# A hybrid decoder block on one Trainium2 core: moving operands shifted by 64 bytes against the stationary ones

## The chip, the core and the metric

The kernel runs on one NeuronCore of a Trainium2 chip. The metric is the device time of one execution in microseconds (us). The engines are named as in the profile: PE is the matrix engine's matmul stream, PEld its weight loads, DVE the vector engine, ACT the scalar engine, POOL the GpSimd engine, SP the engine that issues most DMAs. SBUF is the on-chip memory of 128 partitions that the engines read their operands from, PSUM the accumulators that PE writes.

## What is computed

One decoder layer on 512 tokens of width 1024, all in float32 (cut to what matters):

```python
h = rmsnorm(x, pre_mix_norm)
q_r, k_r, v_r, g_r, q_s, k_s, v_s, gate_r, gate_s = split(h @ w_in)
y_r = (silu(g_r) * group_norm(retention(q_r, k_r, v_r))) @ w_ret_out
y_s = sliding_window_attention(q_s, k_s, v_s, sinks) @ w_swa_out
merged = sigmoid(gate_r) * y_r + sigmoid(gate_s) * y_s
x = x + rmsnorm(merged @ w_out, post_mix_norm)
h = rmsnorm(x, pre_mlp_norm)
u = square(relu(h @ w_up))                  # the MLP's first product, 1024 -> 4096
x = x + rmsnorm(u @ w_down, post_mlp_norm)  # the MLP's second product, 4096 -> 1024
```

## The kernel before

Every float32 operand of a large product is held as two tiles, a high part (`whi`, `hT0`, `h2c0`, ...) and a low part (`wlo`, `hT1`, `h2c1`, ...), of the type float32r. ACT makes the high part by a copy (L129), DVE the low part by a subtraction (L130). A product of two such pairs is three matmuls (`mm3`, L170 to L175): high by high, high by low, low by high.

```python
170    def mm3(ps, a, b, first, last, more=False):
172        (ah, al), (bh, bl) = a, b
173        nc.tensor.matmul(ps, ah, bh, start=first, stop=False, ...)
174        nc.tensor.matmul(ps, ah, bl, start=False, stop=False, ...)
175        nc.tensor.matmul(ps, al, bh, start=False, stop=last, ...)
```

In each of them `a` is the left operand, a block of 128 columns that is loaded into the array (the profile's LDWEIGHTS, on PEld), and `b` the right or moving operand, whose 256 or 512 columns then stream through it (the MATMUL, on PE). The profile names the moving operand first: `wino<-h2c,whi` is a matmul with moving operand `h2c` and stationary operand `whi`.

The stages, in the order of the program:

1. Projections of the input, attention and retention, 0 to 231 us. `pblk` and `ptok` multiply the input `xg` or the normed input `hT`. `wide` (L602) computes two of the projections with Strassen-Winograd's seven products in place of eight: there the left operands are blocks of `hT` and of the four sums over blocks of `hT`, `hsum` (made once, in `wino_tokens`, L183 to L197), and the right operands are weights of 512 columns. Four of its seven products use `hsum`.
2. The two gates and the output product of the retention (`yr`), 231 to about 355.5 us. A gate (`wino_pair`, L241 to L286, eight calls) is again seven products of 4 x 3 matmuls, here with the weights on the left and 256 columns of the tokens on the right: `hT` in three products, `hsum` in four.
3. The product with `w_out`, up to 400.8 us, with the norms between the sub-layers beside and behind it.
4. The MLP's first product, 400.8 to about 570.7 us. The first three of 16 column blocks are done plainly (`up_half`, L1011), each with moving operands `h2c`, `h2b` and `h2d`, the transposed quarters of the normed activations. The other 13 go through `wino_pair` with `h2c` and `h2d` in three products and the sums `h2s` in four.
5. The MLP's second product (`p`, `p4c`), up to 729 us, with 512 columns at a time; its operands are `left` (stationary) and `whi`, `wlo` (moving).

In `wino_pair` the products stand in a fixed order, and the weights of the next pair are prepared while the present one runs: ACT and DVE split the loaded block (`whi`, `wlo`), two sums are formed on DVE (L223, L224), split in their turn into `p24` (the profile's `p`), and so on. Some of these pieces are held back until ACT has copied a certain PSUM bank (L259, L270, L277), so that the preparation follows PE. The first use of `p24` is the product `s2 t2` (L268), the third of a pair, with moving operand `h2s` in the MLP.

Tiles come out of pools. A pool is a stretch of each partition's memory, and its tiles lie one behind the other in the order of their creation; pools opened later lie behind it (or, with `side="right"`, before it from the far end). So where a tile begins is a matter of everything that was made before it. In the kernel before, a tile `pad` of 72 floats (L303) stands at the far end. In the built program these are the starts of the operand tiles, in bytes of the partition, modulo 512:

```
xg, hT, hsum, wkv, whi, wlo, p24, p22, retT, swaT, wo, mhi, mlo,
h2c, h2b, h2d, h2s, left, tch, rb, s (probabilities), retn, zg     192
pt, kd, qc, st, qk (the retention's own tiles)                     448
ident (the identity, moving operand of the transposes)             128
```

Every slice of these tiles that a matmul reads begins a multiple of 512 bytes further in (256 for one operand of the attention), so the numbers hold for the operands of nearly all matmuls.

Of the kernel before, what the change touches and what calls it, by code (L numbers as in the profile page):

```python
# [10 lines left out]
F32 = mybir.dt.float32  # L11
# [5 lines left out]
P = 128  # L17
# [77 lines left out]
def block_kernel(ctx, tc, x, xT, pre_mix, w_in, w_v, w_g, w_gate, w_ret, w_swa, w_out, sinks, post_mix,  # L95
# [9 lines left out]

    def bank(shape, name="ps"):
        return psum.tile(shape, F32, tag="ps", name=name)

    ident = const.tile([P, P], F32, name="ident")
    make_identity(nc, ident)  # L110
# [69 lines left out]
    def wino_pool(stack, side="left"):  # L180
        return stack.enter_context(tc.tile_pool(name="wx", bufs=1, side=side))
# [59 lines left out]
    def wino_pair(wx, a, b, out, then=None):  # L241

        chain = bank([P, 256], "wino")
        p25 = bank([P, 2, 256], "wino")
        p3 = bank([P, 256], "wino")

        def product(ps, x, y, first=True):  # L250
# [39 lines left out]
    hctx = ExitStack()  # L290
    hpool = hctx.enter_context(tc.tile_pool(name="hpool", bufs=1))
    hT = [hpool.tile([P, KD, SEQ], F32R, name=f"hT{i}") for i in range(2)]
    hsum = [hpool.tile([P, 4, 4, 256], F32R, name=f"hsum{i}") for i in range(2)]

# [3 lines left out]
    sctx = ExitStack()  # L300

    side = ctx.enter_context(tc.tile_pool(name="side", bufs=1, side="right"))
    side.tile([P, 72], F32, name="pad")  # L303
    xTpool = sctx.enter_context(tc.tile_pool(name="xTpool", bufs=1, side="right"))
    xTs = xTpool.tile([P, KD, SEQ], F32, name="xTs", tag="xs")
    xgctx = ExitStack()
# [590 lines left out]

    wctx = ExitStack()
    wpool = wctx.enter_context(tc.tile_pool(name="wpool", bufs=1))
    mctx = ExitStack()  # L900
    mpool = mctx.enter_context(tc.tile_pool(name="mpool", bufs=16))
    fctx = ExitStack()
# [90 lines left out]
    uctx = ExitStack()  # L993
    h2pool = uctx.enter_context(tc.tile_pool(name="h2pool", bufs=1))
    h2spool = uctx.enter_context(tc.tile_pool(name="h2spool", bufs=1))
    h2c = [h2pool.tile([P, 2, 4, 256], F32R, name=f"h2c{i}") for i in range(2)]
    h2d = [h2spool.tile([P, 4, 256], F32R, name=f"h2d{i}") for i in range(2)]
    h2s = [h2spool.tile([P, 4, 4, 256], F32R, name=f"h2s{i}") for i in range(2)]
    rspool = uctx.enter_context(tc.tile_pool(name="rspool", bufs=1))
    px = uctx.enter_context(tc.tile_pool(name="px", bufs=1))  # L1000
    wx = wino_pool(uctx)
    pctx = ExitStack()
    ppool = pctx.enter_context(tc.tile_pool(name="ppool", bufs=1))
    h2b = [ppool.tile([P, 4, 256], F32R, name=f"h2b{i}") for i in range(2)]
    quads = [
        [tuple(a[:, 0] for a in h2c), tuple(h2b)],
# [148 lines left out]

    stream2 = ctx.enter_context(tc.tile_pool(name="stream2", bufs=1))
    junks = ctx.enter_context(tc.tile_pool(name="junks", bufs=4))
    ring = ctx.enter_context(tc.tile_pool(name="ring", bufs=2))
    fin = ctx.enter_context(tc.tile_pool(name="fin", bufs=2))

# [193 lines left out]
```

## Time and profile before

| | |
|---|---|
| times of the three runs | 731.77 (median), 730.77, 1835.65 us |
| the profiled execution | 730.93 us, of which the span from first to last instruction is 729.2 us |
| granted TensorE clock in it | 0.998 |

A row of the timeline has the start of an instruction, its duration, engine, line and operation, and the operands. The duration of a MATMUL is modelled and holds the latency from its start to its last result, which overlaps the next ones; what a matmul costs in a stream is the distance from its start to the start of the next.

### The profile page before, as it was taken

To read this page: it belongs to the slowest core of one execution; us is meant where nothing else is said; L and a number is where in the kernel's file an instruction comes from. 1 tells how busy PE (TensorE), PEld (TensorE's weight loads), DVE (VectorE), ACT (ScalarE), POOL (GpSimd) and SP (SyncE) were. 2 spreads that over 40 slices of the span, in tenths; PEclk is the share of its full clock that TensorE was granted. 3 is DMA by queue.
4 is the path that set the end of the run, shared out by engine and by line. 5 is a ranking of instruction groups with operands and counts; after the bars stand their busy time and mean duration, and the time that the engine had idled before them with its cause. 6 is when DMAs were issued, how large, how long until landed. Compare 5 with 4: busy or idle time off the path is not lost.

```text
span 729.2 us, 11245 instructions
## 1 busy us (share of the span) xinstructions
PE 719.3 (99%) x4438; PEld 642.6 (88%) x4438; DVE 535.0 (73%) x808; ACT 423.4 (58%) x712; POOL 59.7 (8%) x75
## 2 busy tenths in 40 slices
PE   8999999999999999999999999999999999999996
PEld 8888888888888999989888999999999888888885
DVE  5599976677975756566944866677676788987797
ACT  6657675445665534435634865766667756556471
POOL 0200000211100000000011100100000010010010
PEclk9999999999999999999999999999999999999999
DMA  9954434907444546543661619766753899699603
GB/s 329 330 166 91 95 83 150 276 8 145 87 144 117 145 116 181 151 132 116 220 243 58 160 48 284 199 175 167 200 146 117 268 291 235 158 199 204 116 1 116
DMA packets 43605, 117.79 MB, mean 162 GB/s; under 512 B 3488, under 2 KB 21024, under 8 KB 37408
## 3 DMA queue, kind: packets, MB, share of 16 engines
q1 hardware_dynamic: 36784, 80.76, 31.5%
q0 software_dynamic: 6480, 36.18, 26.6%
q8 instruction: 35, 0.57, 0.3%
q10 hardware_dynamic: 288, 0.14, 0.1%
q14 instruction: 18, 0.15, 0.1%
HBM read 114.96 MB, written 2.10 MB: 161 GB/s over the span
## 4 chain that ended last, share of the span: by engine, by line
PE 67%; DVE 4%; DMA 2%; issue 1%; ACT 1%; POOL 1%; POOLq 0%; DVEq 0%; ACTq 0%
PE wino L174 10%; PE wino L175 10%; PE wino L173 10%; PE p L173 5%; PE p L174 5%; PE p L175 5%; PE yr L173 2%; PE yr L174 2%; PE ps L175 2%; PE ps L173 2%; PE yr L175 2%; PE ps L174 2%; DVE wlo L130 2%; PE up L175 2%; PE up L173 2%; PE up L174 2%
## 5 line engine op out<-in xcount | busy, mean ns | idle before, releaser
L130 DVE TENSOR_TENSOR wlo<-raw,whi 128x1024 fp32r<-128x1024 f32 x81 | 98.6, 1222 | 49.1 <-ACT whi L129 49.0
L129 ACT CAST whi<-raw 128x1024 fp32r<-128x1024 f32 x81 | 84.7, 1051 | 37.4 <-DMA raw<-in_w_down 7.6
L174 PE MATMUL p<-wlo,left 128*128 128x512 f32 x216 | 84.2, 390 | 0.0
L175 PE MATMUL p<-whi,left 128*128 128x512 f32 x216 | 84.2, 390 | 0.0
L173 PE MATMUL p<-whi,left 128*128 128x512 f32 x216 | 84.0, 390 | 0.1
L175 PEld LDWEIGHTS p<-whi,left 128*128 128x128 f32 x216 | 40.5, 188 | 9.1 <-DVE left L130 0.7
L174 PEld LDWEIGHTS p<-wlo,left 128*128 128x128 f32 x216 | 40.5, 188 | 8.8 <-DVE wlo L130 0.4
L173 PEld LDWEIGHTS p<-whi,left 128*128 128x128 f32 x216 | 40.5, 188 | 8.7 <-ACT left L129 0.5
L130 DVE TENSOR_TENSOR wlo<-tch,whi 128x1024 fp32r<-128x1024 f32 x32 | 38.6, 1218 | 7.1 <-ACT whi L129 7.1
L129 ACT CAST left<-uc 128x1024 fp32r<-128x1024 f32 x28 | 29.3, 1051 | 23.4 <-PE p L174 22.0
L130 DVE TENSOR_TENSOR left<-uc,left 128x1024 fp32r<-128x1024 f32 x28 | 34.1, 1220 | 10.5 <-ACT left L129 10.5
L129 ACT CAST p<-rs 128x1024 fp32r<-128x1024 f32 x21 | 22.1, 1050 | 31.2 <-DVE rs L224 31.2
L129 ACT CAST whi<-tch 128x1024 fp32r<-128x1024 f32 x32 | 33.2, 1050 | 11.4 <-PE p L175 6.8
L130 DVE TENSOR_TENSOR p<-rs,p 128x1024 fp32r<-128x1024 f32 x21 | 25.7, 1225 | 14.7 <-ACT p L129 14.7
L130 DVE TENSOR_TENSOR wlo<-rs,whi 128x1024 fp32r<-128x1024 f32 x21 | 25.7, 1223 | 10.5 <-ACT whi L129 8.5
L173 PE MATMUL wino<-h2c,whi 128*128 128x256 f32 x104 | 29.4, 283 | 0.0
L174 PE MATMUL wino<-h2c,whi 128*128 128x256 f32 x104 | 29.4, 283 | 0.0
L175 PE MATMUL wino<-h2c,wlo 128*128 128x256 f32 x104 | 29.4, 283 | 0.0
L175 PE MATMUL wino<-h2s,p 128*128 128x256 f32 x104 | 29.4, 283 | 0.0
L173 PE MATMUL wino<-h2s,whi 128*128 128x256 f32 x104 | 29.4, 283 | 0.0
L174 PE MATMUL wino<-h2s,whi 128*128 128x256 f32 x104 | 29.4, 283 | 0.0
L175 PE MATMUL wino<-h2s,wlo 128*128 128x256 f32 x104 | 29.4, 283 | 0.0
(354 smaller groups left out, 2330.5 us busy)
## 6 DMA issues: line engine op xcount, KB each, us to landing
tch<-in_w_down POOLq DMA_DIRECT2D x12, 1024.0 KB, 9.2
raw<-in_w_down SPq DMA_DIRECT2D x7, 1024.0 KB, 7.6
rs<-in_w_up SPq DMA_DIRECT2D x13, 512.0 KB, 4.2
rs<-in_w_up POOLq DMA_DIRECT2D x13, 512.0 KB, 5.5
raw<-in_w_up SPq DMA_DIRECT2D x13, 512.0 KB, 5.1
raw<-in_w_in SPq DMA_DIRECT2D x8, 512.0 KB, 5.3
acc<-in_w_v POOLq DMA_DIRECT2D x4, 1024.0 KB, 8.3
rs<-in_w_gate SPq DMA_DIRECT2D x8, 512.0 KB, 3.9
```

What stands on the lines that cost most here:

```text
L129: last["hi"] = nc.scalar.copy(hi, src)
L130: last["split"] = nc.vector.tensor_tensor(lo, src, f(hi), op=ALU.subtract)
L173: nc.tensor.matmul(ps, ah, bh, start=first, stop=False, skip_group_check=more)
L174: nc.tensor.matmul(ps, ah, bl, start=False, stop=False, skip_group_check=more)
L175: nc.tensor.matmul(ps, al, bh, start=False, stop=last, skip_group_check=more)
```

## The change

All instructions of all five engines stand in the same order with the same operands before and after; the only thing that differs is where tiles begin. A helper adds tiles that nothing uses:

```diff
+    def pad(pool, size):
+        pool.tile([P, size // 4], F32, name="pad", bufs=1)
...
     hT = [hpool.tile([P, KD, SEQ], F32R, name=f"hT{i}") for i in range(2)]
+    pad(hpool, 64)
     hsum = [hpool.tile([P, 4, 4, 256], F32R, name=f"hsum{i}") for i in range(2)]
+    hpool.tile([P, 112], F32, name="pad2")
...
-    side.tile([P, 72], F32, name="pad")
+    pad(side, 288)
...
     wpool = wctx.enter_context(tc.tile_pool(name="wpool", bufs=1))
+    pad(wpool, 512)
...
+    pad(h2pool, 64)
     h2c = [h2pool.tile([P, 2, 4, 256], F32R, name=f"h2c{i}") for i in range(2)]
     h2d = [h2spool.tile([P, 4, 256], F32R, name=f"h2d{i}") for i in range(2)]
     h2s = [h2spool.tile([P, 4, 4, 256], F32R, name=f"h2s{i}") for i in range(2)]
     rspool = uctx.enter_context(tc.tile_pool(name="rspool", bufs=1))
+    pad(rspool, 448)
...
     ppool = pctx.enter_context(tc.tile_pool(name="ppool", bufs=1))
+    pad(ppool, 64)
     h2b = [ppool.tile([P, 4, 256], F32R, name=f"h2b{i}") for i in range(2)]
...
     junks = ctx.enter_context(tc.tile_pool(name="junks", bufs=4))
+    pad(junks, 512)
```

The pad of 288 bytes is the same as the 72 floats before. In the built program `hsum`, `h2c`, `h2d`, `h2s` and `h2b` now begin at 256 modulo 512. All other tiles of the table keep their number modulo 512: the pads of 448 (64 + 448 = 512) and 512 bytes put what lies behind at another address but at the same place modulo 512.

```
                 before   after
hT                192      192     (unchanged: pblk, three products of a gate, three of wide)
hsum              192      256     (four products of a gate: moving; four of wide: stationary)
h2c h2d h2s h2b   192      256     (the MLP's first product: moving)
whi wlo p24 p22   192      192     (the stationary operands beside them)
```

## The prediction

> **What bounds the kernel now.** I read first the page's span, its busy times and the chain that ended last.
>
> ```profile
> span 729.2 us, 11245 instructions
> PE 719.3 (99%) x4438; PEld 642.6 (88%) x4438; DVE 535.0 (73%) x808; ACT 423.4 (58%) x712; POOL 59.7 (8%) x75
> PE 67%; DVE 4%; DMA 2%; issue 1%; ACT 1%; POOL 1%; POOLq 0%; DVEq 0%; ACTq 0%
> ```
>
> PE is busy all the time. Then the busy times by stretch, for the two stages in which the shifted tiles are moving operands: the gates (first row: length, then PE, PEld, DVE, ACT and POOL with counts) and the MLP's first product.
>
> ```profile
> 231.40:345.00 113.60, 113.60 (x819) 107.88 (x818) 72.70 (x96) 51.20 (x85) 4.36 (x5) 1.00 0.48 134
> 437.30:570.50 133.20, 133.20 (x1102) 132.50 (x1100) 94.33 (x120) 88.29 (x155) 10.50 (x12) 1.00 0.66 178
> ```
>
> PE never stands idle there, at the full granted clock, and DVE and ACT have a quarter or more of the time to spare. So the time of these stages is the number of matmuls times the distance between their starts, and whatever changes that distance goes into the end of the kernel one for one. That distance is the only thing that an address can change here, since no instruction, order or wait differs.
>
> The distance is read from the timeline. First 256 columns (52 starts in a row, of a gate), then 512 columns (28 starts, of the MLP's second product):
>
> ```profile
> 299.76 0.28 PE L175 MATMUL wino<-hsum,wlo 128*128 128x256 f32 x1
> ...
> 305.88 0.28 PE L175 MATMUL wino<-hT,wlo 128*128 128x256 f32 x1
> ```
> ```profile
> 599.73 0.39 PE L174 MATMUL p<-wlo,left 128*128 128x512 f32 x1
> ...
> 605.85 0.39 PE L174 MATMUL p<-wlo,left 128*128 128x512 f32 x1
> ```
>
> The first pair of rows holds 51 distances: 6.12 / 51 = 0.1200 us. The second holds 27: 6.12 / 27 = 0.2267 us. The further 256 columns cost 106.7 ns, or 0.417 ns a column. So 256 columns by themselves would take 106.7 ns, and each matmul has **13.3 ns** on top, at either width. The weight loads lie beside the matmuls, one for each:
>
> ```profile
> 300.01 0.19 PEld L175 LDWEIGHTS wino<-hsum,wlo 128*128 128x128 f32 x1
> 300.13 0.19 PEld L173 LDWEIGHTS wino<-hsum,whi 128*128 128x128 f32 x1
> ```
>
> The next load begins about 0.01 us after a matmul has begun (300.00 and 300.01), so both read SBUF at the same time: the present moving operand and the next stationary one. Before the change both begin at 192 modulo 512 bytes. The 13.3 ns are all that the change can take away, and the question is whether they come of these two reads meeting at the same place.
>
> **The change, part by part.** It adds no instruction. Its pads of 288, 448 and 512 bytes leave every other tile at its place modulo 512; I cost these at nothing, as no read that goes on at the same time as another changes its relation to it. What moves in phase is the moving operand of these matmuls (the rows of L173; L174 and L175 have the same counts):
>
> ```profile
> L173 PE MATMUL wino<-hsum,p x64: 283/283/283, 234.2 to 344.3; 128*128 128x256 f32 x64
> L173 PE MATMUL wino<-hsum,whi x64: 283/283/283, 237.0 to 342.8; 128*128 128x256 f32 x64
> L173 PE MATMUL wino<-h2c,whi x104: 283/283/283, 437.3 to 560.8; 128*128 128x256 f32 x104
> L173 PE MATMUL up<-h2c,whi x48: 278/283/283, 400.8 to 419.7; 128*128 128x256 f32 x48
> L173 PE MATMUL wino<-h2s,p x104: 277/283/283, 440.2 to 570.5; 128*128 128x256 f32 x104
> L173 PE MATMUL wino<-h2s,whi x104: 283/283/283, 443.1 to 566.6; 128*128 128x256 f32 x104
> L173 PE MATMUL wino<-h2d,p x52: 283/283/283, 441.6 to 563.7; 128*128 128x256 f32 x52
> L173 PE MATMUL up<-h2d,whi x24: 283/283/283, 421.5 to 437.0; 128*128 128x256 f32 x24
> L173 PE MATMUL up<-h2b,whi x24: 283/283/283, 420.0 to 435.5; 128*128 128x256 f32 x24
> L173 PE MATMUL wide<-whi,hsum x64: 388/389/501, 62.4 to 199.8; 128*128 128x512 f32 x64
> ```
>
> 3 x (64 + 64 + 104 + 48 + 104 + 104 + 52 + 24 + 24) = **1764 matmuls** of 256 columns, 211.7 us of the span at 0.1200. Besides, 192 matmuls of 512 columns in `wide` have `hsum` on the left.
>
> What a shift by 64 bytes does, the trace does not show; rows near it bound it. A shift by 256 bytes does nothing: in the retention `whi` (192) moves while `pt` (448) is loaded, with some matmuls of two operands at 448 between, and 13 distances make 1.56 us, 0.1200 each:
>
> ```profile
> 160.35 0.28 PE L175 MATMUL ret_v<-whi,pt 128*128 128x256 f32 x1
> ...
> 161.91 0.28 PE L173 MATMUL ret_v<-whi,pt 128*128 128x256 f32 x1
> ```
>
> The one kind with 64 bytes between its operands is the transposes: `ident` (128) moves, `s` (192) is loaded. Eleven of them take 1.20 us, 0.1091 each:
>
> ```profile
> 84.17 0.60 PE L475 MATMUL psd<-ident,s 128*128 128x128 f32 x4
> 84.60 0.49 PE L477 MATMUL psp<-ident,s 128*128 128x128 f32 x3
> 84.93 0.60 PE L475 MATMUL psd<-ident,s 128*128 128x128 f32 x4
> 85.37 0.49 PE L477 MATMUL psp<-ident,s 128*128 128x128 f32 x3
> ```
>
> If a transpose of 128 columns goes through at half the rate (106.7 ns, my reading, which no row proves), only 2.4 ns lie on top in place of 13.3. It is another kind of instruction, so this is weak. That the 13.3 ns are not fixed, two places show: after a matmul of 512 columns the first two distances are 0.11 and 0.12, and after a wait six distances make 0.71 us, 0.118 each:
>
> ```profile
> 262.35 0.28 PE L173 MATMUL wino<-hT,whi 128*128 128x256 f32 x1
> 262.46 0.28 PE L174 MATMUL wino<-hT,whi 128*128 128x256 f32 x1
> 262.58 0.28 PE L175 MATMUL wino<-hT,wlo 128*128 128x256 f32 x1
> ```
> ```profile
> 411.65 0.28 PE L175 MATMUL up<-h2c,wlo 128*128 128x256 f32 x1
> ...
> 412.36 0.28 PE L175 MATMUL up<-h2c,wlo 128*128 128x256 f32 x1
> ```
>
> So the part on top depends on how the two reads stand to each other in time. That is what two reads that get in each other's way would do, and nothing that is fixed in the array would. I take it that the shift removes a part. The lower end of the distance is 0.1091 (the transposes' 2.4 ns on top), the upper, where it does harm, 0.1253 (below). Between, the nearest rows are those of the same instruction outside its steady state, 0.11 and 0.118; I take a little under their upper one, **0.115**. The sum: 1764 x (0.1200 - 0.1150) = 8.8 us off. The 192 matmuls of `wide` go in at 0 (from -192 x 13.3 ns = -2.6 us to 192 x 5.3 ns = +1.0 us), since there the stationary operand is shifted and the trace says nothing of the sign. Against the profiled execution: 730.93 - 8.8 = 722.1, told as **722 us**. (The median of the runs is 0.84 us above the profiled one, which the rounding covers.)
>
> What would come due next? The tightest preparation is in every fourth pair, where DVE has an extra subtraction: ACT's copy of a finished bank, then sums and splits, then the first use of `p`.
>
> ```profile
> 495.12 0.37 ACT L277 COPY uc<-wino 128x256 f32<-128x256 f32 x1 [1.04 <-PE wino L175]
> 499.04 1.23 DVE L130 TENSOR_TENSOR p<-rs,p 128x1024 fp32r<-128x1024 f32 x1 [1.12 <-ACT p L129]
> 500.68 0.28 PE L173 MATMUL wino<-h2s,p 128*128 128x256 f32 x1
> ```
>
> `p` is done at 500.27, 0.41 us ahead of its use. Between copy and use lie four products, 48 matmuls, so PE would begin to wait below 0.1200 - 0.41 / 48 = 0.1115. At 0.115 nothing comes due; at 0.1091 three of 13 pairs would wait some 0.1 us each.
>
> A rule of the Trainium skill speaks against all this. "TensorE: Matmul & The Clock Gate", section "Step-by-step: what each phase is for", has two independent SBUF read ports, one for the moving operand and one for the weights, so that loading the next weights takes nothing from the running matmul; by it the shift is worth nothing, 730.9 us. The Trainium skill's same page, section "Wait — 56ns, not 53.3ns?", gives a warm matmul about 2.5 ns over its columns; that is an estimate of 109.2 ns for 256 columns. The trace has 120.0 with a load beside every matmul, so something of 10.8 ns remains that these two places do not name.
>
> **The rivals.** (1) *Nothing changes.* The 13.3 ns are a cost of changing weights, whatever the addresses. For it: they are the same at 256 and 512 columns, in every stage, and at a shift of 256 bytes. And if both reads run on through many lines at different speeds, a shifted start only moves the meetings. Against it: the distances of 0.11 and 0.118. Time: 730.9 us. (The two read ports of the Trainium skill's page on TensorE lead here.) That the pads do not move the tiles is excluded by the built program's addresses.
>
> (2) *All of it goes.* The two reads meet at one place only, and 64 bytes part them: 0.1091, 1764 x 10.9 ns = 19.2 us, less 0.3 for the three pairs that wait: 712.0 us. For it: the transposes. Against it: they are another instruction, and no float32r stream in the trace runs at this distance.
>
> (3) *Slower.* The steady 0.1200 and 0.2267 are a state in which the two reads, started at the same phase, have fallen into step, and 64 bytes break it. What a stream out of step costs stands behind a wait in the second product: five distances of 512 columns make 1.16 us, 0.2320 in place of 0.2267, before it falls back.
>
> ```profile
> 641.32 0.39 PE L175 MATMUL p<-whi,left 128*128 128x512 f32 x1
> 641.55 0.40 PE L173 MATMUL p<-whi,left 128*128 128x512 f32 x1
> 641.79 0.39 PE L174 MATMUL p<-wlo,left 128*128 128x512 f32 x1
> 642.01 0.62 PE L175 MATMUL p<-whi,left 128*128 128x512 f32 x2
> 642.48 0.39 PE L173 MATMUL p<-whi,left 128*128 128x512 f32 x1
> ```
>
> 5.3 ns on 1764 matmuls are 9.3 us, and 1.0 in `wide`: 741.2 us. It would be over 2% from 8.8 ns on. Against it: at 256 columns the stream out of step is the quicker one (0.118).
>
> **How the numbers follow.** Forecast (a part goes, distance 0.111 to 0.119, 715 to 729 us) 0.40; nothing 0.32; all 0.10; slower 0.18. Within 2% (717 to 746 us) is about what a measurement of this kernel can't tell from no change. Faster by over 2% needs a distance below about 0.112: all of rival 2 and a quarter of the forecast, 0.20. Slower by over 2% needs 8.8 ns: a third of rival 3, 0.06. The rest, 0.74, lies between. The range for 8 in 10 reaches from just below rival 2 to just above rival 3's price, 711 to 742 us.
>
> **What would show it.** In the profile after, the starts of `wino<-h2c`, `wino<-h2s` and `wino<-hsum` rows would follow each other every 0.115 us, those of `wino<-hT`, which keep their phase, still every 0.120; the stretch from the first `up` to the last `wino` of the MLP would shrink by 1380 x 5 ns = 6.9 us, the gates by 1.9, all else by nothing. The forecast is wrong if the shifted rows stay at 0.120 (rival 1), reach 0.109 (rival 2) or rise (rival 3); and its reason is wrong if the `hT` rows move as well.

## The result, and the profile after

| | before | after |
|---|---|---|
| median of 13 runs each | 731.66 us | 727.97 us |
| ratio after to before, with its 95% interval | | 0.9941 [0.9927, 0.9956] |
| the profiled execution | 730.93 us | 728.88 us |

One of the 13 runs before (1835.65 us) and one of `mlp_back64` below (784.78 us, its granted clock 0.85) are slow ones, which the ratios leave out. The change makes the kernel 3.7 us (0.6%) faster. The forecast was 722 us: the direction was right, and so was the step that the distance depends on the shift; the size was less than half of what was forecast. The times after stand in two groups with nothing between: eleven from 727.4 to 729.1 us and two at 723.4 and 723.7 us. The experiments come back to this.

The lines of L173 to L175 are L177 to L179 now, since four lines were added above them. The page's span and busy times of the kernel after:

```profile
span 727.1 us, 11246 instructions
PE 716.7 (99%) x4438; PEld 638.5 (88%) x4438; DVE 535.2 (74%) x808; ACT 422.1 (58%) x712; POOL 59.8 (8%) x75
```

PE is as full as before, and the same 4438 matmuls take 2.6 us less. The busy times of the MLP's first product without `up` (length, then PE, PEld, DVE, ACT and POOL with counts, clock, DMA share):

```profile
437.40:568.70 131.30, 131.29 (x1105) 130.52 (x1105) 95.02 (x120) 86.95 (x155) 10.49 (x12) 1.00 0.67 181
```

PE is still busy all the time, at the full clock, and the stretch is shorter by 2 us (131.3 against 133.2). The timeline of PE shows why. First a window of the MLP after, 54 rows with the two shown:

```profile
479.74 0.28 PE L178 MATMUL wino<-h2c,whi 128*128 128x256 f32 x1
...
485.98 0.28 PE L177 MATMUL wino<-h2s,p 128*128 128x256 f32 x1
```

6.24 us / 53 = 0.1177 us from start to start, where it was 0.1200. In the gates both kinds of rows stand side by side:

```profile
296.21 0.28 PE L179 MATMUL wino<-hT,wlo 128*128 128x256 f32 x1
...
297.05 0.28 PE L177 MATMUL wino<-hsum,p 128*128 128x256 f32 x1
...
299.91 0.28 PE L177 MATMUL wino<-hsum,whi 128*128 128x256 f32 x1
...
302.39 0.28 PE L177 MATMUL wino<-hsum,whi 128*128 128x256 f32 x1
```

Seven distances of `hT`, which kept its place, make 0.84 us, 0.1200 each; 21 distances of `hsum`, which moved, make 2.48 us, 0.1181 each. So each tile's own shift decides over its own rows.

In `wide`, where `hsum` is the stationary operand and the moving one has 512 columns, the same 24 matmuls of the first group, before and after:

```profile
62.43 0.39 PE L173 MATMUL wide<-whi,hsum 128*128 128x512 f32 x1
...
67.64 0.39 PE L175 MATMUL wide<-whi,hsum 128*128 128x512 f32 x1
```
```profile
61.41 0.40 PE L177 MATMUL wide<-whi,hsum 128*128 128x512 f32 x1
...
66.78 0.40 PE L179 MATMUL wide<-whi,hsum 128*128 128x512 f32 x1
```

5.21 / 23 = 0.2265 before, 5.37 / 23 = 0.2335 after: here the change costs time.

The sum over the stages of the two profiled executions, by first and last starts of their matmuls: the MLP's first product 2.80 us less (`up` 0.46, the rest 2.34), the gates 0.27 less, the six groups of `wide` with `hsum` 0.85 more; everything else together 0.1 more. The spans differ by 2.1 us. The medians differ by 3.7: the profiled execution of before is 0.7 us under its median, that of after 0.9 us over its own. So 2.1 of the 3.7 us are found in rows. The rest is not assigned: the time up to the first gate alone, with the same places modulo 512, is 230.7 to 232.7 us in the six profiles that have `hsum` unshifted at the full clock, and the two short runs pull the median after down (that of the other eleven is 728.6 us).

**Where the gates' gain went.** Their 384 `hsum` rows at about 0.118 should give 0.8 us. Of that, 0.47 us were lost in two new short waits, ahead of the first `wino<-hsum,p` at 250.88 and at 312.93. The second of them after, by ACT's and PE's rows:

```profile
311.56 1.05 ACT L133 CAST whi<-raw 128x1024 fp32r<-128x1024 f32 x1 [1.58 <-DMA raw<-in_w_gate]
...
312.51 0.36 ACT L281 COPY sgs<-wino 128x256 f32<-128x256 f32 x1
...
312.93 0.19 PEld L177 LDWEIGHTS wino<-hsum,p 128*128 128x128 f32 x1 [0.24 <-ACT sgs L281]
```

A weight transfer lands late, ACT's cast starts late, the copy that empties a PSUM bank stands behind the cast on ACT, and PE's next product needs that bank. The same place before, in its ACT rows and the first weight load and matmul of that product:

```profile
310.63 1.05 ACT L129 CAST whi<-raw 128x1024 fp32r<-128x1024 f32 x1 [1.31 <-DMA raw<-in_w_gate]
...
311.58 0.37 ACT L277 COPY sgs<-wino 128x256 f32<-128x256 f32 x1
...
312.01 0.19 PEld L173 LDWEIGHTS wino<-hsum,p 128*128 128x128 f32 x1
312.12 0.28 PE L173 MATMUL wino<-hsum,p 128*128 128x256 f32 x1
```

There the copy was done at 311.95, 0.06 us ahead of the load. Where PE waits it is the load that waits: it begins 52 ns after the copy's end in the kernel after and in `mlp_256`. Before it began 56 ns after it. So there was all but nothing to spare, and a transfer that lands some tenths later makes PE wait. It needs no shift: the kernel `mlp_256` below, whose matmuls are no quicker than before's, waits at the same place:

```profile
312.25 0.19 PEld L177 LDWEIGHTS wino<-hsum,p 128*128 128x128 f32 x1 [0.34 <-ACT sgs L281]
```

The wait comes and goes with the transfers: of the profiles with `hsum` unshifted, `h2b_in_step` has it at the earlier of the two places, and `mlp_only` has none. A quicker PE comes nearer to it (36 matmuls at 2 ns less are some 0.07 us), but that the change brought these two waits is not shown.

### The profile page after: what moved, and what is told of

Same layout as the page of the kernel before. It is cut to its first block, busy times and chain, and to the rows that moved or that the text cites. A ratio compares the mean times of both kernels' runs of the same rounds, so it can differ in the third digit from the quotient of the medians.

```text
span 727.1 us, 11246 instructions
## 1 busy us (share of the span) xinstructions
PE 716.7 (99%) x4438; PEld 638.5 (88%) x4438; DVE 535.2 (74%) x808; ACT 422.1 (58%) x712; POOL 59.8 (8%) x75
## 5 line engine op out<-in xcount | busy, mean ns | idle before, releaser
L179 PE MATMUL p<-whi,left 128*128 128x512 f32 x216 | 84.1, 390 | 0.1
L177 PE MATMUL p<-whi,left 128*128 128x512 f32 x216 | 84.0, 390 | 0.1
L179 PEld LDWEIGHTS p<-whi,left 128*128 128x128 f32 x216 | 40.5, 188 | 9.3 <-DVE left L134 0.9
L177 PEld LDWEIGHTS p<-whi,left 128*128 128x128 f32 x216 | 40.5, 188 | 8.8 <-ACT left L133 0.5
L179 PE MATMUL wino<-h2c,wlo 128*128 128x256 f32 x104 | 29.1, 280 | 0.0
L179 PE MATMUL wino<-h2s,wlo 128*128 128x256 f32 x104 | 29.1, 280 | 0.0
L179 PE MATMUL wino<-h2s,p 128*128 128x256 f32 x104 | 29.1, 280 | 0.0
L177 PE MATMUL wino<-h2s,p 128*128 128x256 f32 x104 | 29.0, 279 | 0.0
L178 PE MATMUL wino<-h2s,p 128*128 128x256 f32 x104 | 29.0, 279 | 0.0
L177 PE MATMUL wino<-h2c,whi 128*128 128x256 f32 x104 | 29.0, 279 | 0.0
```

Source lines behind the costliest of these rows:

```text
L177: nc.tensor.matmul(ps, ah, bh, start=first, stop=False, skip_group_check=more)
L178: nc.tensor.matmul(ps, ah, bl, start=False, stop=False, skip_group_check=more)
L179: nc.tensor.matmul(ps, al, bh, start=False, stop=last, skip_group_check=more)
```

## The experiments

The theory: the distance depends on how the addresses of the moving operand and of the weights that are loaded meanwhile stand to each other, and 64 bytes are worth what the kernel after shows at 256 columns (2.2 ns less) and at 512 (some 7 ns more). Rivals: it depends on the absolute place of one operand; it is the pads or the tiles' new addresses as such; or the distance is settled by what ran just before.

**The shift alone, swept.** A kernel of matmuls only, which leaves the whole layer out: one stationary tile `left` and moving tiles that begin 0 to 480 bytes further, 72 matmuls for each.

```diff
+    for n in (256, 512):
+        for o in (0, 32, 64, 96, 128, 160, 192, 224, 256, 288, 320, 384, 448, 480):
+            for i in range(72):
+                nc.tensor.matmul(ps[:, :n], left[:, (i % 8) * P : (i % 8 + 1) * P], moving[o][:, i % 4, :n], ...)
```

> A kernel of matmuls alone: blocks of 72 float32r matmuls, the stationary operand always at one phase, the moving operand 0, 32, 64, ... 480 bytes further modulo 512, first with 256, then with 512 columns. Its output is not the layer's. Theory (two reads that meet, decided by the phase): 0.1200 us at 0 and 256 bytes and 0.2267 at 512 columns, as in the kernel before; 0.118 at 64 bytes with 256 columns, as in the kernel after, and longer than 0.2267 with 512 columns; other offsets differ among each other, with one period. Rival (the place in the program, the data or the order of the operands makes the difference, not the phase): the same distance at all offsets for each width.

The timeline of PE, one row for each block (`m064b` begins 64 bytes after `left`); the distance is the time to the next row's start, divided by 72:

```profile
44.48 8.65 PE L44 MATMUL acc<-m064b,left 128*128 128x256 f32 x72
52.96 8.79 PE L44 MATMUL acc<-m096b,left 128*128 128x256 f32 x72
61.59 8.71 PE L44 MATMUL acc<-m128b,left 128*128 128x256 f32 x72
...
78.58 8.64 PE L44 MATMUL acc<-m192b,left 128*128 128x256 f32 x72
87.06 8.68 PE L44 MATMUL acc<-m224b,left 128*128 128x256 f32 x72
95.58 8.80 PE L44 MATMUL acc<-m256b,left 128*128 128x256 f32 x72
104.21 8.65 PE L44 MATMUL acc<-m288b,left 128*128 128x256 f32 x72
...
129.72 8.35 PE L44 MATMUL acc<-m448b,left 128*128 128x256 f32 x72
137.91 8.68 PE L44 MATMUL acc<-m480b,left 128*128 128x256 f32 x72
146.42 16.53 PE L44 MATMUL acc<-m000b,left 128*128 128x512 f32 x72
162.79 16.97 PE L44 MATMUL acc<-m032b,left 128*128 128x512 f32 x72
179.59 16.65 PE L44 MATMUL acc<-m064b,left 128*128 128x512 f32 x72
196.09 16.97 PE L44 MATMUL acc<-m096b,left 128*128 128x512 f32 x72
...
346.53 16.96 PE L44 MATMUL acc<-m448b,left 128*128 128x512 f32 x72
363.32 16.96 PE L44 MATMUL acc<-m480b,left 128*128 128x512 f32 x72
```

At 256 columns 64 bytes give 8.48 / 72 = 117.8 ns, 96 bytes 119.9, 256 bytes 119.9 again, 448 bytes 113.8 (113.3 once the block has settled). At 512 columns no shift gives 227.4 (226.7 settled), 32 bytes 233.3, 64 bytes 229.2, 448 bytes 233.2. What follows: the shift alone gives the kernel's 117.8 ns; not every shift gains (96 bytes cost what none costs); and the two widths want opposite things, for at 512 columns every shift that was tried and isn't a multiple of 256 bytes is worse than none. In `wide` after the change the moving operand lies 64 bytes behind the stationary one, so its rows of 0.2335 go with the 233.2 at 448 bytes, not with the 229.2 at 64. The period is 256 bytes: at 256 columns the blocks of 32, 64, 128 and 224 bytes come out again 256 bytes further within 0.1 ns. One pair does not: 192 bytes gave 8.48 / 72 = 117.8 and 448 bytes 113.8. The kernel `history` below takes that up.

**Each half of the change alone.** In `mlp_only` the pad ahead of `hsum` is gone, in `hsum_only` those ahead of the MLP's tiles.

```diff
 mlp_only
-    pad(hpool, 64)
-    hpool.tile([P, 112], F32, name="pad2")
+    hpool.tile([P, 128], F32, name="pad2")
 hsum_only
-    pad(h2pool, 64)
-    pad(rspool, 448)
+    pad(rspool, 512)
-    pad(ppool, 64)
```

> The change without the shift of hsum, which stays at 192 modulo 512; all other tiles lie where they lie after the change. Theory (each shifted 256-column matmul gains 2.2 ns, each 512-column matmul of wide with hsum on the left loses some 6 ns): the MLP keeps its 1380 x 2.2 = 3.0 us, the gates give back 0.3, wide gets its 1.2 to 2.0 us back: 727.0 to 728.0 us where before is 731.7, a ratio of 0.994 to 0.995, at or a little below the change's own. Rival (the gain is made elsewhere, by the addresses of all tiles or by when the first transfers land): as the change, and the MLP's stretch is not the part that is shorter.

> The change with the shift of hsum alone; h2c, h2d, h2s and h2b stay at 192 modulo 512. Theory: wide loses 192 x 6 = 1.2 us, the gates gain 384 x 2.2 = 0.8 us less what the switches between hT and hsum cost: 0.5 to 1.5 us over before, a ratio of 1.000 to 1.002. Rival (the gain is made elsewhere): about the change's time, 0.994.

`mlp_only`: 727.87 us against 731.17, ratio 0.9931 [0.9905, 0.9956]; its MLP is 2.78 us shorter, gates and `wide` are as before. `hsum_only`: 731.16 against 731.17, ratio 0.9995 [0.9973, 1.0017]; its gates are 0.61 us shorter, its first group of `wide` with `hsum` stands at 0.2335, and the six groups are 1.1 us longer. The 0.5 to 1.5 us over before that were expected do not show in the median. So the MLP's tiles carry the gain, and what the shift of `hsum` does to the whole time is too small to tell. Three of eleven runs of `mlp_only`, too, lie apart, at 722.5 to 723.5 us.

**What ran before.** The matmuls-only kernel again, with blocks of 72 at 64, 192 and 160 bytes, each entered from ten different things.

> Matmuls alone again, its output is not the layer's: blocks of 72 with 256 columns and the moving operand 64, 192 or 160 bytes further than the stationary one, each entered from ten different things (24 or 25 matmuls of 512 or 256 columns in phase, others out of phase, eight transposes, a wait). Theory (two reads in step: one phase has more than one steady state, and what ran before picks it): at 192 bytes some blocks at 0.1178 and some at 0.1133, and the same in some blocks at 64. Rival (the phase alone sets the distance, and the 0.1133 of the offset 448 belongs to 448 and not to 192): every block of 64 and of 192 at 0.1178, every block of 160 at 0.1173.

The timeline of PE, some blocks at 192 bytes (64 short of the next 256) and what they were entered from:

```profile
147.41 8.64 PE L46 MATMUL acc<-m192b,left 128*128 128x256 f32 x72
155.89 5.83 PE L46 MATMUL acc<-m000b,left 128*128 128x512 f32 x25
161.56 8.64 PE L46 MATMUL acc<-m192b,left 128*128 128x256 f32 x72
170.04 3.04 PE L46 MATMUL acc<-m000b,left 128*128 128x256 f32 x24
172.91 8.34 PE L46 MATMUL acc<-m192b,left 128*128 128x256 f32 x72
181.09 3.14 PE L46 MATMUL acc<-m000b,left 128*128 128x256 f32 x25
```

Entered from 512 columns in phase, a block takes 8.48 us (117.8 ns each); entered from 256 columns in phase, 8.18 us (113.6, settling at 113.3). The same instruction on the same addresses has **two steady distances**, and it keeps the one that it fell into for the whole block. At 192 bytes five of ten entries gave the shorter one, at 64 bytes one of ten; blocks of 160 bytes settle at 117.3 to 117.4 or at 118.6 to 118.8. The sweep's pair of 192 and 448 bytes fits this. The kind of entry alone does not decide: behind 72 matmuls of 256 columns at 384 bytes (128 modulo 256) the sweep's block of 448 went to 113.3, and behind 24 at 128 bytes the block of 192 here went to 117.8. That is what the two groups of times would come of: 1092 matmuls of the MLP x 4.4 ns = 4.8 us, and the groups lie 4 to 5 us apart.

**Which operand counts.** A third kernel of matmuls only has two stationary tiles, `left` and, 64 bytes further, `shifted`, each beside moving tiles at 0, 64 and 128 bytes.

> Matmuls alone, its output is not the layer's: two stationary operands, the second 64 bytes behind the first, each with moving operands at 0, 64 and 128 bytes from the first; also 4, 16, 48, 80 and 112 bytes with the first alone; at last 512 columns with the two stationary operands in turn. Theory (the distance between the two operands counts, modulo 256): the second stationary operand with the moving one at 64 gives 0.1200 and 0.2267, with 128 gives 0.1178 (or 0.1133) and 0.2289, with 0 gives 0.1178 or 0.1133 and 0.2333. Rival (the moving operand's own place counts): both stationary operands give the same three numbers.

The timeline of PE at 256 columns, a row for each block (and the start of the next):

```profile
89.89 8.64 PE L50 MATMUL acc<-m000b,shifted 128*128 128x256 f32 x72
98.38 8.79 PE L50 MATMUL acc<-m064b,shifted 128*128 128x256 f32 x72
107.01 8.65 PE L50 MATMUL acc<-m128b,shifted 128*128 128x256 f32 x72
115.49 16.50 PE L50 MATMUL acc<-m000b,left 128*128 128x512 f32 x72
```

With `shifted` it is the moving tile at 64 bytes that takes the long 8.63 us (119.9 ns each), and those at 0 and 128, 64 bytes off on either side, take 8.48 or 8.49. At 512 columns the three settle at 233.3, 226.7 and 228.9 ns, as the theory has it. At these places the absolute place of neither operand matters, only the difference. The small shifts with `left` settle at 123.3 ns (4 bytes), 116.7 (16), 118.3 (48), 120.0 (80) and 113.3 (112) with 256 columns, and at 236.7, 231.7, 233.3, 231.1 and 231.1 with 512. So a shift can also cost at 256 columns: 3.3 ns at 4 bytes.

**Places other than 64 bytes, in the kernel.** `mlp_256` shifts the MLP's tiles by 256 bytes, `mlp_back64` by 448, so that they begin 64 bytes short of a multiple of 256 further; `hsum` is unshifted in both.

Against `mlp_only`:

```diff
 mlp_256
-    pad(h2pool, 64)
+    pad(h2pool, 256)
-    pad(rspool, 448)
+    pad(rspool, 256)
-    pad(ppool, 64)
+    pad(ppool, 256)
 mlp_back64
-    pad(h2pool, 64)
+    pad(h2pool, 448)
-    pad(rspool, 448)
+    pad(rspool, 64)
-    pad(ppool, 64)
+    pad(ppool, 448)
```

> The moving operands of the MLP's first product shifted by 256 bytes in place of 64, everything else as in the kernel with the MLP's shift alone. Theory (phase modulo 256 bytes): every distance in the MLP at 0.1200, 731.2 us, ratio 1.000. Rival (another address or a pad between the tiles is enough): 727.9 us, 0.994 to 0.995.

> The moving operands of the MLP's first product at 128 modulo 512, 64 bytes behind the stationary ones in place of 64 ahead; hsum unshifted. Theory (only the phase counts, and this one has the two steady states 0.1178 and 0.1133): 1380 x 2.2 to 6.7 = 3.0 to 9.2 us off the time before, 722.0 to 728.2 us, ratio 0.987 to 0.996. Rival (the shift has to be forward, or the gain came of the addresses as such): no gain, 731.

`mlp_256`: 731.72 us against 731.66, ratio 0.9995 [0.9974, 1.0015]. The timeline of its PE, 52 rows with the two shown:

```profile
479.80 0.28 PE L178 MATMUL wino<-h2c,whi 128*128 128x256 f32 x1
...
485.92 0.28 PE L178 MATMUL wino<-h2s,whi 128*128 128x256 f32 x1
```

6.12 / 51 = 0.1200: pads and other addresses alone do nothing. `mlp_back64`: runs at 722.9, 723.0, 727.2, 727.8 and 728.3 us against 731.66, ratio 0.992 [0.9893, 0.9947]: the two groups once more. The same kernel a second time, for a profile:

> The kernel with the MLP's moving operands 64 bytes behind once more, for a profile at the full clock. Theory: the Winograd pairs of the MLP run either all at 0.1178 (727.5 us) or, from some point on, at 0.1133 (723 us); nothing lies between for long. Rival (the runs at 723 us are shorter by something outside the MLP, such as the first transfers): the MLP at 0.1178 in a run of 723 us.

722.8 to 724.5 us in all four runs, ratio 0.9896 [0.9883, 0.9908]. The timeline of PE in the profiled one (723.13 us), 55 rows with the two shown:

```profile
479.79 0.28 PE L177 MATMUL wino<-h2d,p 128*128 128x256 f32 x1
...
485.91 0.28 PE L177 MATMUL wino<-h2c,whi 128*128 128x256 f32 x1
```

6.12 / 54 = 0.1133. The MLP's stretch behind `up` is 126.42 us there, 131.08 in the kernel after; the gates and the second product are as in the other kernels. `h2b_in_step` and `hsum_back64` below, of 725.10 and 722.66 us, are at 0.1133 in the MLP too, and `mlp_only` (727.59 us) is at 0.1178. So the runs near 723 us are those with the shorter of the two distances. That the two such runs of the change itself are of this kind follows from their time alone: none of them was profiled.

**Choosing the distance.** If an entry from 256 columns in phase leads to the shorter distance at -64 bytes, the kernel can be made to fall into it: `h2b`, whose matmuls alternate with those of `h2d` in `up`, twelve by twelve, goes back to its old place. `h2b_in_step_fwd` is the same with the other tiles at +64, where the matmul-only kernel nearly always gave 117.8.

```diff
 mlp_back64 -> h2b_in_step
-    pad(ppool, 448)
 mlp_only -> h2b_in_step_fwd
-    pad(ppool, 64)
```

> The MLP's moving operands 64 bytes behind the stationary ones as before, but h2b left in phase: the twelve matmuls with h2b run ahead of each twelve with h2d, and the last of these lead into the Winograd pairs. Theory (the quicker of the two steady states is entered out of the stream in phase, as in the matmul kernel, where both blocks of 192 bytes entered from 24 or 25 matmuls in phase ran at 0.1133): all or nearly all runs in the quicker state, the Winograd pairs at 0.1133: 1092 x 6.7 = 7.3 us and some 0.6 in the plain blocks, 723.8 us, ratio 0.989. Rival (which state a run takes is chance): some runs at 723 and more at 728, as without this.

> As the kernel with h2b in step, but the other moving operands of the MLP 64 bytes ahead, as in the change, in place of 64 behind. Theory (the state is picked by the stream before and the direction): in the matmul kernel the blocks of 64 bytes ahead that were entered out of 24 or 25 matmuls in phase ran at 0.1178, never at 0.1133; so all runs in the slower state, 1092 x 2.2 and some 0.3 in the plain blocks: 729 us, ratio 0.996, and no run near 723. Rival (leaving h2b in phase brings the quicker state by itself, whatever the direction): 724 us as with 64 behind.

`h2b_in_step`: 722.9 to 725.1 us in five runs, ratio 0.9893 [0.9875, 0.991]. The timeline of its PE in the profiled execution (725.10 us), at the entry from `h2b` to `h2d` and on (10 rows from 437.11 to 438.13, 56 rows from 479.73 to 485.96):

```profile
436.63 0.28 PE L179 MATMUL up<-h2b,wlo 128*128 128x256 f32 x1
436.75 0.29 PE L177 MATMUL up<-h2d,whi 128*128 128x256 f32 x1
...
437.11 0.28 PE L177 MATMUL up<-h2d,whi 128*128 128x256 f32 x1
...
438.13 0.28 PE L177 MATMUL wino<-h2c,whi 128*128 128x256 f32 x1
...
479.73 0.28 PE L178 MATMUL wino<-h2s,p 128*128 128x256 f32 x1
...
485.96 0.28 PE L179 MATMUL wino<-h2c,wlo 128*128 128x256 f32 x1
```

`h2b` is in phase, `h2d` at -64; three matmuls after the change the distance is 1.02 / 9 = 0.1133, and forty us later still 6.23 / 55 = 0.1133. `h2b_in_step_fwd`: 727.8 to 730.6 us, none near 723, ratio 0.9968 [0.9956, 0.998], its rows at 0.1178. The sign of the shift counts: by their times, 15 of the 18 runs at -64 that are compared here (`hsum_back64` below included) are at the shorter distance, and 5 of 30 at +64. What `h2b` in phase adds is less sure. At -64 all nine runs with it are at the shorter distance and six of nine without it; at +64 none of six and five of 24. That is the way the theory has it, but chance could do it too.

**The best of it.** `hsum_back64` is `h2b_in_step` with `hsum`, too, 64 bytes short.

```diff
 h2b_in_step -> hsum_back64
+    pad(hpool, 448)
-    hpool.tile([P, 128], F32, name="pad2")
+    hpool.tile([P, 16], F32, name="pad2")
```

> The same, and hsum 64 bytes back too, at 128 modulo 512. Theory: the gates gain up to 384 x 6.7 = 2.6 us less the entry of each product, some 2.2; in wide, where hsum is stationary, the moving operand is then 64 ahead, 0.2289 in place of 0.2267, 192 x 2.2 = 0.4 us lost: 722.0 us, ratio 0.987. Rival (the switches between products eat the gates' gain, as with the change): 724 us, as without it.

722.64 us against 731.66, ratio 0.9875 [0.986, 0.989], the shortest median of all. Its PE in a gate, 24 rows with the two shown:

```profile
301.16 0.28 PE L177 MATMUL wino<-hsum,whi 128*128 128x256 f32 x1
...
303.77 0.28 PE L179 MATMUL wino<-hsum,p 128*128 128x256 f32 x1
```

2.61 / 23 = 0.1135. The gates are 1.7 us shorter than before, although PE waits twice for the bank there as well (0.7 us); the six groups of `wide` with `hsum` are 0.2 us longer.

## Why the prediction was right or wrong

- *PE sets the end, and the distance goes into it one for one.* Right but for one wait. The MLP's 1380 matmuls at 2.2 ns less make 3.0 us, and the stage lost 2.80. Some 0.1 of the rest is a wait that grows with PE's speed: among the last matmuls of the MLP stand ten of the second product, which wait for DVE's `left`, and the third distance among them is 0.31 us before, 0.41 after and 0.56 where the MLP is at 0.1133.
- *The 13.3 ns come of the two reads and depend on the shift.* That they depend on the shift is right, and by more than one kernel: 256 bytes do nothing, the kernel of two stationary tiles shows the difference alone to count, and rows of `hT` beside those of `hsum` keep 0.1200. That all of the 13.3 come of the two reads is not shown: no shift took off more than 6.7.
- *The distance is 0.115.* This is the step that failed. The rows near it were 0.11 and 0.118; the prediction took "a little under their upper one", and it measured 0.1178, the upper row itself. The 0.118 was the one row of six distances in sequence; the 0.11 was a single first distance after a change of width, and the middle between the two describes neither. With 0.1178 the sum would have been 1764 x 2.2 = 3.9 us, 727.0 us. What the prediction did not foresee at all is that there are two steady distances, 0.1178 and 0.1133, on either side of its 0.115, of which the change, by its times, falls into the longer in eleven runs of 13. The other two, at 723.4 and 723.7 us, lie near the forecast of 722 by luck: they belong to a distance that the prediction did not have.
- *`wide` at 0, at most 1.0 more.* It cost 0.85 us: inside the bound, at its unfavourable end. The price was in the prediction's own rival 3, whose rows of 512 columns out of step were longer; but there it came only together with longer rows of 256 columns, which are shorter here, and the forecast left it at nothing.
- *`hT` rows stay at 0.120.* Right for the steady rows.
- *What comes due next.* The chain of `p` in the MLP did not come due at 0.1178, as the prediction said, and PE does not wait for it at 0.1133 either. But the time to spare was read up to the matmul, and the load that needs `p` begins before it, at 500.57: 0.30 us, not 0.41. It is 0.22 in the kernel after and 0.45 at 0.1133, so it does not shrink along the prediction's line; why it grows again was not followed. The one that did stand close was elsewhere: the bank behind ACT's cast in the gates, emptied 0.06 us ahead of the load, which the prediction had not looked at. It took 0.47 us of the profiled execution.
- *Rival 1, nothing changes.* Refuted by the MLP's rows. The Trainium skill's rule ("TensorE: Matmul & The Clock Gate", section "Step-by-step: what each phase is for") that loading the next weights takes nothing from the running matmul does not account for them: here the distance changes from 120.0 to 117.8 or 113.3 ns with the two addresses alone.
- *Rival 2, all of it goes.* 0.1091 was reached by no shift that was tried; 0.1133 was the least.
- *Rival 3, slower.* Right for 512 columns, wrong for 256 at 64 bytes; a shift of 4 bytes is slower there too (123.3 ns). Its "over 2% from 8.8 ns on" should be 8.3 ns: 2% of 730.93 us are 14.6 us, over 1764 matmuls. Only the chance of 0.06 hangs on it.

What the two reads meet at was not shown: the runs give the times by address, width and history, and the cause behind them stays open. Why a single execution of one and the same program falls into the one or the other distance was not settled either, only that the sign of the shift moves the odds and that, in the kernels of matmuls alone, one shift gave both distances behind different streams.

## What to carry to other kernels

Where PE is full and every matmul comes with a weight load, lay the moving operand out against the weights on purpose: for 256 float32r columns 64 bytes short of a multiple of 256 was the best here (113.3 ns in most runs), for 512 columns a multiple of 256. Check a tile that is moving in one product and stationary in another on both sides. Where a trace offers two rows for an unknown steady distance, take the one that is steady over several instructions, and not a value between. Ahead of a gain in one stage, look in each stage which buffer has the least time to spare, counted up to the load that waits for it; here it was a bank that was emptied 0.06 us ahead, behind a cast that waited for a transfer.

## What the hardware showed beyond that

- One stream of equal matmuls has two steady distances on equal addresses (117.8 and 113.3 ns at a shift of 64 or 192 bytes), and stays in the one that it entered: for 1080 of the MLP's 1092 matmuls in a row, up to ten matmuls of 512 columns.
- The two signs of a shift are not alike: entered from 256 columns in phase, the three blocks of -64 bytes went to 113.3 ns and the three of +64 bytes to 117.8.
- At 512 columns the operands in phase are the best (226.7 ns), and every other shift that was tried in steps of 32 bytes within 256 costs 2 to 8 ns.
- A shift of only 4 bytes is slower than none at both widths: 123.3 against 120.0 ns and 236.7 against 226.7.
